# Hybrid attention and mLSTM layer: tiles at other addresses modulo 256, and all output products 256 columns wide

## The chip, the cores and the metric

The kernel runs on one core of one Trainium2 chip. TensorE (PE) multiplies matrices from SBUF into PSUM; VectorE (DVE), ScalarE (ACT) and GpSimd (POOL) do the rest; SyncE (SP) issues most DMAs. The metric is the device time of one execution in microseconds (us), taken as the median of several runs.

## What is computed

One decoder layer over 256 tokens of width 1024, all in 32-bit floats:

```python
h = rmsnorm(x, g_pre)
q_a, k_a, v_a, g_a, x_m, z_m = split(h @ w_in)      # 1024 x 6144, six parts of 1024 columns
y_a = attention(q_a, k_a, v_a, rel_bias) * silu(g_a)            # 8 heads of 128, causal
x_c = silu(conv4(x_m) + conv_b)                                 # depthwise, 4 taps
q_m, k_m, v_m = blockdiag(x_c, wq), blockdiag(x_c, wk), blockdiag(x_m, wv)
h_m = headwise_layernorm(mlstm(q_m, k_m, v_m, gates))           # 4 heads of 256
y_m = (h_m + skip * x_c) * silu(z_m)
out = x + rmsnorm(concat(y_a, y_m) @ w_out, g_post)             # 2048 x 1024
```

With 256 tokens and attention blocks of 256, attention is plain causal attention with a bias by distance.

## The kernel before

**Products in three terms.** The two large projections multiply numbers split in two: `hi` is a value rounded to the type fp32r and `lo` is the rest, and a product is the sum of three: hi x hi, hi x lo, lo x hi. The weights come in 32 blocks of 128 x 2048 (24 of `w_in`, 8 of `w_out`), each by one DMA into a `raw` tile; ACT rounds it into `hi` (line 101), DVE subtracts into `lo` (line 111), in halves, some blocks ahead (`split_next`). Each of `raw`, `hi` and `lo` has three buffers.

**The input projection.** The first two blocks arrive in pieces together with x and are multiplied in `project_group` (line 580). The other 22 go through `project` (line 566): for each half m of a block, 24 products (3 terms x 8 row blocks), each with its own weight load of 128 x 128 and 256 moving columns. For most blocks the stationary operand is the weight (`hi` or `lo`) and the moving one the input (`hhi`, `hlo`); for the v blocks it is the other way round.

**Small products between them.** `evacuate` and the generators started with `spawn` run between the halves: every half is a slot, `run_side` lets each generator do its next step before the half's products are issued. So PE's order is written by hand: a few small products, then 24 projection products. The names in the profile: `vps` and `qps` (lines 331, 338) make the mLSTM's v and q from the convolution; `gp`, `gif`, `cp` (351, 358, 385) its gates; `sp`, `nps`, `ht` (395 to 443) its heads; `as` (460, 461) the attention scores, `atp` (480) their transposes, `ao` (491, 492) the attention's output. `nps` and the first three products of `ao` have fp32r operands, the other small ones four-byte floats, which PE takes in two instructions each (transposes in one).

**The output projection.** `multiply_out(j, p)` (line 667) multiplies two of the 16 row blocks into one of five PSUM banks. `pieces` gives each bank its 128 tokens and columns: three are 512 columns wide and two 256. For each of the 2 row blocks there are 3 terms, with the layer's activations (`ymh`, `yml` of the mLSTM half; `yah`, `yal` of attention) stationary and the weights moving. Eight blocks j go through two slots each; the first ones still have attention steps between them. At the end `finish` takes the mean square of each bank (ACT, DVE) and the root (POOL), and `store` scales, adds x and writes out.

**Where tiles lie.** SBUF tiles come from four pools laid one behind the other: `cst`, `wts`, `wrk`, `big`. Inside a pool a tile (or a tag, which several tiles use in turn) takes the next address in the order of first request, rounded up to 32 bytes. `pad(n)` requests n bytes in `cst` that nothing uses. Every slice that a projection product reads starts a multiple of 512 bytes into its tile, so an operand's address modulo 256 is its tile's.

Of the kernel before, what the change touches and what calls it, by code (L numbers as in the profile page):

```python
# [10 lines left out]
F32 = mybir.dt.float32  # L11
F32R = mybir.dt.float32r
AF = mybir.ActivationFunctionType
OP = mybir.AluOpType
# [3 lines left out]
P = 128  # L18
D = 1024
S = 256  # L20
# [29 lines left out]
def hybrid_layer(ctx, tc, x, xw, small, wide, bias_t, g_post, w_in, w_out, out):  # L50
    nc = tc.nc
    pe, act, dve, pool = nc.tensor, nc.scalar, nc.vector, nc.gpsimd
# [5 lines left out]
    def pad(n):  # L58
        cst.tile([P, n // 4], F32, name="pad%d" % n)
# [7 lines left out]
    def bank(name):  # L67
        return psm.tile([P, 512], F32, tag="bank", name=name)
# [4 lines left out]
    def half_kb(name, n):  # L73
        return wrk.tile([P, n], F32, tag="kb2", name=name, bufs=6)
# [40 lines left out]

    big = ctx.enter_context(tc.tile_pool(name="big", bufs=1))

    first = big.tile([P, 6144 + 8], F32, name="first")  # L120

    def third(i):
        return first[:, 2048 * i:2048 * (i + 1)].rearrange("p (k s) -> p k s", s=S)
# [41 lines left out]
    gcol = first[:, 6144:]  # L165
    xc = third(1)

    sq = big.tile([P, 4, 2, S], F32, tag="ym0", name="sq")
    part = big.tile([P, S], F32, tag="ym1v", name="part")

    def rms_squares(q):
# [35 lines left out]
    rcol = cst.tile([P, 2], F32, name="rcol")  # L207
# [21 lines left out]
    def rms_spread(dg):  # L229
# [6 lines left out]
    bd = big.tile([P, 16, P], F32R, tag="ym0", name="bd").bitcast(F32)  # L236
    bda, bdv = bd[:, 0:8, :], bd[:, 8:16, :]
    bias = None
    xms = (big.tile([P, 6, S + 3], F32, tag="xm", name="xma"),
           big.tile([P, 2, S + 3], F32, tag="xmv", name="xmb"))  # L240

    def xm(f, n=1):
        t, f = (xms[0], f) if f < 6 else (xms[1], f - 6)
        return t[:, f, :] if n == 1 else t[:, f:f + n, :]

    v1h = big.tile([P, 2, MH, EH + 2], F32R, tag="v1", name="v1h")
    v1l = big.tile([P, 2, MH, EH + 2], F32R, name="v1l")

    tmp = big.tile([P, 1280], F32, tag="ym1", name="tmp")
    tmpv = big.tile([P, 576], F32, tag="ym1v", name="tmpv")  # L250

    wkr = tmp[:, 0:128]
    wifr = tmp[:, 128:896].rearrange("p (i n) -> p i n", i=3)
# [39 lines left out]
    def spawn(gen, at):  # L293
        side.append([at, gen])
# [15 lines left out]
    def conv(c, ps):  # L310
        dve.tensor_tensor(xm(2 * c, 2)[:, :, 3:], ps, rb2, OP.mult)
        yield CONV[c]
        cv = half_kb("cv", 512).rearrange("p (i n) -> p i n", n=S)
        for i in range(2):
            f = 2 * c + i
            act.activation(cv[:, i], xm(f)[:, 0:S], AF.Copy, scale=cols[:, 8 + f:9 + f])
        yield 1
        for i in range(2):
            f = 2 * c + i
            for j in range(1, 4):  # L320
                dve.scalar_tensor_tensor(cv[:, i], xm(f)[:, j:j + S],  # L321
                                         cols[:, 8 + 8 * j + f:9 + 8 * j + f], cv[:, i],
                                         op0=OP.mult, op1=OP.add)
            yield 1
            act.activation(xc[:, f, :], cv[:, i], AF.Silu, bias=cols[:, 40 + f:41 + f])  # L325
        yield VWAIT
        vps = bank("vps").rearrange("p (t n) -> p t n", n=EH)
        for t in range(2):
            for i in range(2):
                f = 2 * c + i  # L330
                pe.matmul(vps[:, t, i * P:(i + 1) * P], xm(f)[:, 3 + t * P:3 + (t + 1) * P],  # L331
                          bdv[:, f, :], start=True, stop=True)
        act.copy(v1h[:, :, c, 0:EH], vps)
        yield 1
        dve.tensor_tensor(v1l[:, :, c, 0:EH], vps, v1h[:, :, c, 0:EH].bitcast(F32), OP.subtract)
        qps = bank("qps").rearrange("p (a n) -> p a n", n=S)
        for i in range(2):
            pe.matmul(qps[:, i, :], bda[:, 2 * c + i, :], xc[:, 2 * c + i, :], start=True, stop=True)  # L338
        act.copy(qp[:, 2 * c:2 * c + 2, :], qps)

    pad(576)

    def row(name):
        return cst.tile([MH, S], F32, name=name)
# [103 lines left out]

    gs, yah = {}, {}
    yal = cst.tile([P, 8, S], F32R, name="yal")  # L450
    ym = {}
    gq = {}
    rb2 = rbc.unsqueeze(1).to_broadcast([P, 2, S])

    def attend(h):
        g, v0 = gq[h // 2]
        qt, kt, v1 = g[:, 0:2], g[:, 2:4], g[:, 4]
        i = h % 2
        sp = bank("as")
        pe.matmul(sp[:, 0:S], qt[:, i, P:], kt[:, i, :], start=True, stop=True)  # L460
        pe.matmul(sp[:, S:384], qt[:, i, 0:P], kt[:, i, 0:P], start=True, stop=True)  # L461
        e = half_kb("ae", 384)
        mn = wrk.tile([P, 2], F32, name="amn")
        rs = wrk.tile([P, 2], F32, name="ars")
        parts = ((0, 0, S), (1, S, 384))
        for a, o, z in parts:
            dve.tensor_tensor_reduce(e[:, o:z], sp[:, o:z], bias[:, h, S - (z - o):], -1.0, 3.0e38,  # L467
                                     OP.add, OP.min, mn[:, a:a + 1])
        yield 1
        for a, o, z in parts:  # L470
            act.activation(e[:, o:z], e[:, o:z], AF.Exp, scale=-1.0, bias=mn[:, a:a + 1],
                           accum_out=rs[:, a:a + 1])
        yield 1
        dve.reciprocal(rs, rs)
        for a, o, z in parts:
            dve.tensor_scalar(e[:, o:z], e[:, o:z], rs[:, a:a + 1], None, op0=OP.mult)
        yield 1
        tp = bank("atp")
        for n, o in enumerate((S, 0, P)):
            pe.transpose(tp[:, n * P:(n + 1) * P], e[:, o:o + P], ident)  # L480
        pt = wrk.tile([P, 2, S], F32R, tag="gsplit", name="apt", bufs=PBUF)
        p1 = half_kb("ap1", P)
        act.copy(pt[:, 0], tp[:, 0:S])  # L483
        act.copy(p1, tp[:, S:384])
        yield 1
        dve.tensor_tensor(pt[:, 1], tp[:, 0:S], pt[:, 0].bitcast(F32), OP.subtract)
        yield 1
        op = bank("ao")
        vs = slice(i * P, (i + 1) * P)
        for n, (a, b) in enumerate(((0, 0), (1, 0), (0, 1))):  # L490
            pe.matmul(op[:, 0:S], v0[:, a, vs], pt[:, b], start=n == 0, stop=False)  # L491
        pe.matmul(op[:, P:S], v1[:, vs], p1, start=False, stop=True)  # L492
        y = half_kb("ay", S)
        dve.tensor_tensor(y, op[:, 0:S], gs[h], OP.mult)
        yield 1
        yah[h] = big.tile([P, S], F32R, tag="ya%d" % h, name="yah")
        act.copy(yah[h], y)
        yield 1
        dve.tensor_tensor(yal[:, h, :], y, yah[h].bitcast(F32), OP.subtract)
# [26 lines left out]
    def evacuate(n, ps, slot):  # L526
        kind, c, _ = chunks[n]
        if kind == "m":
            spawn(conv(c, ps), slot)
            if c == 3:  # L530
                spawn(gates(), slot + GATES)
                for h in range(MH):
                    spawn(mlstm_head(h), slot + HEADS + HSTEP * h)
        elif kind == "z":
            spawn(gate_z(c, ps), slot)
        else:
            if kind == "g":
                spawn(gate_a(c, ps), slot)
            elif kind == "q":
                tag = ("ym1", "xm")[c % 2]  # L540
                gq[c] = (big.tile([P, 5, S], F32, tag=tag, name="qkv"),
                         big.tile([P, 2, S], F32R, tag=tag + "v", name="v0"))
                dve.scalar_tensor_tensor(gq[c][0][:, 0:2], ps, P ** -0.5, rb2, op0=OP.mult, op1=OP.mult)
            elif kind == "k":
                dve.tensor_tensor(gq[c][0][:, 2:4], ps, rb2, OP.mult)
            else:
                g, v = gq[c]
                act.activation(v[:, 0], ps[:, 0], AF.Copy, scale=rcol[:, 0:1])
                act.activation(g[:, 4], ps[:, 1], AF.Copy, scale=rcol[:, 1:2])
                dve.scalar_tensor_tensor(v[:, 1], ps[:, 0], rcol[:, 0:1], v[:, 0].bitcast(F32),  # L550
                                         op0=OP.mult, op1=OP.subtract)
                spawn(attend(2 * c), slot + 1)
                spawn(attend(2 * c + 1), slot + ASTEP)
# [60 lines left out]
    for n in range(2, NIN):  # L614
        ps = proj_bank()
# [42 lines left out]
    acc = []  # L658

    def multiply_out(j, p):  # L660
        n = NIN + j
        t, c, w = pieces[p]
        for i in range(2):
            f = (order[j] + i) % 8
            yh, yl = (yah[f], yal[:, f]) if order[j] < 8 else (ym["h"][:, f], ym["l"][:, f])
            for q, (yt, wt) in enumerate(((yh, his[n]), (yl, his[n]), (yh, los[n]))):
                pe.matmul(acc[p][:, 0:w], yt[:, t * P:(t + 1) * P], wt[:, i * D + c:i * D + c + w],  # L667
                          start=j == 0 and i == 0 and q == 0, stop=j == 7 and i == 1 and q == 2)

    steps = [(((j,), (0, 1)), ((j,), (2, 3, 4))) for j in range(6)]  # L670
    steps += [(((6,), (0, 1)), ((7,), (0, 1))), (((6, 7), (2,)), ((6, 7), (3, 4)))]
# [23 lines left out]
    for j in range(8):  # L695
        for m in range(2):
# [3 lines left out]
            if not acc:  # L700
                acc = [bank("acc%d" % p) for p in range(5)]
            js, ps = steps[j][m]
# [113 lines left out]
```

## Time and profile before

| | us |
|---|---|
| median of 3 runs (228.36 to 228.82) | 228.61 |
| the profiled execution | 228.33 |
| its span, first to last instruction | 226.6 |
| PE busy | 219.2 |
| DVE busy | 161.4 |
| ACT busy | 128.2 |
| POOL busy | 29.4 |

The profile is of one execution. A product's listed duration contains its way through the array and overlaps the next one's, so the distance between the starts of two products, or the length of a piece of the chain over its count, tells what a product costs. PE means products and PEld their weight loads.

### The profile page before, as it was taken

To read this page: it belongs to the slowest core of one execution; us is meant where nothing else is said; L and a number is where in the kernel's file an instruction comes from. 1 tells how busy PE (TensorE), PEld (TensorE's weight loads), DVE (VectorE), ACT (ScalarE), POOL (GpSimd) and SP (SyncE) were. 2 spreads that over 40 slices of the span, in tenths; PEclk is the share of its full clock that TensorE was granted. 3 is DMA by queue.
4 is the path that set the end of the run, shared out by engine and by line. 5 is a ranking of instruction groups with operands and counts; after the bars stand their busy time and mean duration, and the time that the engine had idled before them with its cause. 6 is when DMAs were issued, how large, how long until landed. Compare 5 with 4: busy or idle time off the path is not lost.

```text
span 226.6 us, 4213 instructions
## 1 busy us (share of the span) xinstructions
PE 219.2 (97%) x1688; PEld 209.0 (92%) x1688; DVE 161.4 (71%) x321; ACT 128.2 (57%) x228; POOL 29.4 (13%) x49
## 2 busy tenths in 40 slices
PE   8999999999999999999999999999999999999980
PEld 8999999999889999999999999999998888888870
DVE  1787999999935967384698898997773665464163
ACT  4787525877469464552656575996445634432220
POOL 2001394000000212000316154000000000000010
PEclk9999999999999999999999999999999999999996
DMA  6999594244545199425050440455545743740022
GB/s 197 406 420 373 197 353 147 74 178 174 194 179 188 15 302 327 149 90 188 0 189 0 185 159 30 185 188 185 188 187 185 268 140 150 275 187 3 0 93 94
DMA packets 7027, 39.90 MB, mean 176 GB/s; under 512 B 796, under 2 KB 1312, under 8 KB 3040
## 3 DMA queue, kind: packets, MB, share of 16 engines
q1 hardware_dynamic: 6608, 38.65, 46.1%
q0 software_dynamic: 256, 0.79, 1.5%
q8 instruction: 13, 0.21, 0.4%
q10 hardware_dynamic: 144, 0.20, 0.2%
q14 instruction: 6, 0.05, 0.1%
HBM read 38.58 MB, written 1.05 MB: 175 GB/s over the span
## 4 chain that ended last, share of the span: by engine, by line
PE 94%; issue 2%; DVE 1%; ACT 0%; POOLq 0%; POOL 0%; DVEq 0%
PE proj L566 54%; PE acc L667 17%; PE proj L580 5%; PE wake L160 2%; PE nps L416 2%; PE vps L331 2%; PE as L460 2%; PE sp L395 2%; PE qps L338 2%; PE ao L491 1%; PE atp L480 1%; PE gp L351 1%; PE sp L398 1%; PE as L461 1%; PE ao L492 1%
## 5 line engine op out<-in xcount | busy, mean ns | idle before, releaser
L111 DVE TENSOR_TENSOR lo<-raw,hi 128x1024 fp32r<-128x1024 f32 x60 | 72.5, 1225 | 3.3 <-ACT hi L101 3.3
L101 ACT CAST hi<-raw 128x1024 fp32r<-128x1024 f32 x60 | 61.6, 1046 | 12.4 <-issue 7.6
L566 PE MATMUL proj<-hhi,hi 128*128 128x256 f32 x288 | 41.7, 288 | 0.0
L566 PE MATMUL proj<-hlo,hi 128*128 128x256 f32 x288 | 39.5, 280 | 0.0
L566 PE MATMUL proj<-hhi,lo 128*128 128x256 f32 x288 | 39.3, 279 | 0.0
L566 PEld LDWEIGHTS proj<-hhi,hi 128*128 128x128 f32 x288 | 36.4, 189 | 1.0 <-issue 0.8
L566 PEld LDWEIGHTS proj<-hlo,hi 128*128 128x128 f32 x288 | 36.1, 189 | 0.1
L566 PEld LDWEIGHTS proj<-hhi,lo 128*128 128x128 f32 x288 | 36.0, 189 | 0.0
L667 PE MATMUL acc<-hi,ymh 128*128 128x512 f32 (+1 forms) x40 | 14.3, 357 | 0.0
L667 PE MATMUL acc<-hi,yah 128*128 128x512 f32 (+1 forms) x40 | 14.0, 350 | 0.0
L667 PE MATMUL acc<-hi,yml 128*128 128x512 f32 (+1 forms) x40 | 14.0, 350 | 0.0
L667 PE MATMUL acc<-lo,ymh 128*128 128x512 f32 (+1 forms) x40 | 14.0, 350 | 0.0
L667 PE MATMUL acc<-lo,yah 128*128 128x512 f32 (+1 forms) x40 | 14.0, 349 | 0.0
L667 PE MATMUL acc<-hi,yal 128*128 128x512 f32 (+1 forms) x40 | 13.9, 349 | 0.0
L686 POOL TENSOR_TENSOR oms<-oms,nhalf 128x1 f32<-128x1 f32 x2 | 1.1, 567 | 80.4 <-DVE oms L683 80.4
L483 ACT CAST apt<-atp 128x256 fp32r<-128x256 f32 x8 | 3.0, 370 | 13.8 <-PE atp L480 13.4
L325 ACT ACTIVATE first<-cv,sm 128x256 f32<-128x256 f32 x8 | 4.1, 510 | 9.8 <-DVE cv L321 9.8
L438 POOL TENSOR_SCALAR first<-first,sm 128x256 f32<-128x256 f32 x8 | 9.6, 1205 | 0.0
L679 ACT ACTIVATE sq<-acc 128x512 f32<-128x512 f32 (+1 forms) x5 | 2.6, 511 | 12.3 <-PE acc L667 12.3
L467 DVE CUSTOM_DVE_ANT_0 ae<-as,first 128x256 f32<-128x256 f32 (+1 forms) x16 | 5.0, 353 | 5.7 <-PE as L461 5.7
L566 PE MATMUL proj<-hi,hhi 128*128 128x256 f32 x64 | 9.1, 284 | 0.0
L321 DVE SCALAR_TENSOR_TENSOR cv<-xma,sm,cv 128x256 f32<-128x256 f32 x18 | 8.8, 488 | 0.4
(170 smaller groups left out, 388.3 us busy)
## 6 DMA issues: line engine op xcount, KB each, us to landing
raw<-in_w_in_dram SPq DMA_DIRECT2D x22, 1024.0 KB, 4.9
raw<-in_w_out_dram SPq DMA_DIRECT2D x8, 1024.0 KB, 4.8
first<-in_xw_dram SPq DMA_DIRECT2D x2, 768.0 KB, 7.9
first<-in_xw_dram SPq DMA_DIRECT2D x2, 512.0 KB, 5.1
first<-in_bias_dram SPq DMA_DIRECT2D x1, 1024.0 KB, 8.1
first<-in_x_dram SPq DMA_DIRECT2D x1, 1024.0 KB, 7.0
dl<-mdr POOLq DMA_DIRECT2D x1, 512.0 KB, 6.2
go<-in_g_post_dram SPq DMA_DIRECT2D x1, 512.0 KB, 7.8
```

What stands on the lines that cost most here:

```text
L101: act.copy(his[n][:, sl], raws[n][:, sl])
L111: dve.tensor_tensor(los[n][:, sl], raws[n][:, sl], his[n][:, sl].bitcast(F32), OP.subtract)
L160: pe.matmul(wk[:, 0:P], one, one, start=True, stop=True)
L321: dve.scalar_tensor_tensor(cv[:, i], xm(f)[:, j:j + S], cols[:, 8 + 8 * j + f:9 + 8 * j + f], cv[:, i], op0=OP.mult, op1=OP.add)
L331: pe.matmul(vps[:, t, i * P:(i + 1) * P], xm(f)[:, 3 + t * P:3 + (t + 1) * P], bdv[:, f, :], start=True, stop=True)
L338: pe.matmul(qps[:, i, :], bda[:, 2 * c + i, :], xc[:, 2 * c + i, :], start=True, stop=True)
L395: pe.matmul(sp[:, 0:S], xc[:, f, 0:P], qp[:, f, :], start=i == 0, stop=i == 1)
L438: pool.tensor_scalar(u[:, f, :], xc[:, f, :], cols[:, 56 + f:57 + f], None, op0=OP.mult)
L467: dve.tensor_tensor_reduce(e[:, o:z], sp[:, o:z], bias[:, h, S - (z - o):], -1.0, 3.0e38, OP.add, OP.min, mn[:, a:a + 1])
L566: pe.matmul(ps[:, m, :], a, b, start=first and j == ks[0] and k == 0, stop=last and j == ks[-1] and k == KT - 1)
L580: pe.matmul(ps[:, i, :], wt[:, k, i * P:(i + 1) * P], ht[:, k, :], start=k == 0 and i == 0 and j == 0, stop=k == 7 and i == 1 and j == 2, ...
L667: pe.matmul(acc[p][:, 0:w], yt[:, t * P:(t + 1) * P], wt[:, i * D + c:i * D + c + w], start=j == 0 and i == 0 and q == 0, stop=j == 7 and ...
```

## The change

Two things. Gaps of 32 to 224 bytes are put between the tags of `big` (a new helper `big_pad`), one pad of `cst` is cut by 64 bytes and 64 bytes are put behind `yal`; the tile of q, k and v gets 8 unused floats ahead of v (the second half of v's tokens), and `tmp`, which shares its buffer, grows likewise. And in `multiply_out` every product covers 256 columns: a 512-wide one becomes two with the same stationary operand, issued one behind the other.

Addresses modulo 256, added up from the sizes in order of request:

| tile | before | after |
|---|---|---|
| `hhi`, `hlo`; `xc`, `qp` and other parts of `first`; `gsplit`, `apt`; `ident` | 160 | 160 |
| `hi`, `lo`, `raw` | 224 | 224 |
| `sq`, `bd`, `yml` (tag `ym0`) | 192 | 32 |
| `part`, `tmpv`, `v0` of even pairs (tag `ym1v`) | 192 | 224 |
| `xma`, q and k of odd pairs (tag `xm`); `tmp`, q and k of even pairs, `go` (tag `ym1`) | 192 | 192 |
| `xmb`, `v0` of odd pairs (tag `xmv`) | 32 | 224 |
| `v1h`, `ymh` (tag `v1`) | 64 | 32 |
| `v1l` | 128 | 96 |
| `gs`, `yah` (tags `ya0` to `ya7`) | 192 | 32 |
| `yal` | 96 | 32 |
| v of the second half of the tokens, `g[:, 4]` | 192 | 224 |
| small scratch tiles (`ae`, `ap1`, `hn`, ...) | 32 | 32 |

```diff
@@ -115,6 +115,11 @@
+    def big_pad(n, gaps=[]):
+        gaps.append(n)
+        big.tile([P, n // 4], F32, name="gap%d" % len(gaps))
@@ -165,7 +170,9 @@
+    big_pad(96)
     sq = big.tile([P, 4, 2, S], F32, tag="ym0", name="sq")
+    big_pad(192)
     part = big.tile([P, S], F32, tag="ym1v", name="part")
@@ -236,18 +243,23 @@
-    xms = (big.tile([P, 6, S + 3], F32, tag="xm", name="xma"),
-           big.tile([P, 2, S + 3], F32, tag="xmv", name="xmb"))
+    big_pad(224)
+    xma = big.tile([P, 6, S + 3], F32, tag="xm", name="xma")
+    big_pad(192)
+    xms = xma, big.tile([P, 2, S + 3], F32, tag="xmv", name="xmb")
...
+    big_pad(32)
     v1h = big.tile([P, 2, MH, EH + 2], F32R, tag="v1", name="v1h")
     v1l = big.tile([P, 2, MH, EH + 2], F32R, name="v1l")
 
-    tmp = big.tile([P, 1280], F32, tag="ym1", name="tmp")
+    big_pad(32)
+    tmp = big.tile([P, 1288], F32, tag="ym1", name="tmp")
     tmpv = big.tile([P, 576], F32, tag="ym1v", name="tmpv")
+    big_pad(64)
@@ -338,7 +350,7 @@
-    pad(576)
+    pad(512)
@@ -448,13 +460,14 @@
     yal = cst.tile([P, 8, S], F32R, name="yal")
+    pad(64)
...
-        qt, kt, v1 = g[:, 0:2], g[:, 2:4], g[:, 4]
+        qt, kt, v1 = g[0], g[1], g[2]
@@ -538,15 +551,16 @@
-                gq[c] = (big.tile([P, 5, S], F32, tag=tag, name="qkv"),
-                         big.tile([P, 2, S], F32R, tag=tag + "v", name="v0"))
+                g = big.tile([P, 5 * S + 8], F32, tag=tag, name="qkv")
+                gq[c] = ([g[:, o:o + 2 * S].rearrange("p (i s) -> p i s", s=S) for o in (0, 2 * S)] +
+                         [g[:, 4 * S + 8:]], big.tile([P, 2, S], F32R, tag=tag + "v", name="v0"))
...
@@ -664,8 +678,12 @@
-                pe.matmul(acc[p][:, 0:w], yt[:, t * P:(t + 1) * P], wt[:, i * D + c:i * D + c + w],
-                          start=j == 0 and i == 0 and q == 0, stop=j == 7 and i == 1 and q == 2)
+                for o in range(0, w, S):
+                    pe.matmul(acc[p][:, o:o + S], yt[:, t * P:(t + 1) * P],
+                              wt[:, i * D + c + o:i * D + c + o + S],
+                              start=j == 0 and i == 0 and q == 0 and o == 0,
+                              stop=j == 7 and i == 1 and q == 2 and o + S == w,
+                              skip_group_check=True)
```

The lines left out write and read q, k and v through `g[0]`, `g[1]` and `g[2]`.

## Rows read from the trace of the kernel before

**Rows 1.** The page: busy us of each engine, share of the span, instructions.

```profile
PE 219.2 (97%) x1688; PEld 209.0 (92%) x1688; DVE 161.4 (71%) x321; ACT 128.2 (57%) x228; POOL 29.4 (13%) x49
```

**Rows 2.** The page: the chain that ended last, shares by engine and by line.

```profile
PE 94%; issue 2%; DVE 1%; ACT 0%; POOLq 0%; POOL 0%; DVEq 0%
PE proj L566 54%; PE acc L667 17%; PE proj L580 5%; PE wake L160 2%; PE nps L416 2%; PE vps L331 2%; PE as L460 2%; PE sp L395 2%; PE qps L338 2%; PE ao L491 1%; PE atp L480 1%; PE gp L351 1%; PE sp L398 1%; PE as L461 1%; PE ao L492 1%
```

**Rows 3.** Waits of PE: us in total, times, longest.

```profile
PE wake L160 <- PEq L804: 0.8, 1, 0.8
```

**Rows 4.** Timeline after the last product: start us, us, engine, line, operation.

```profile
220.07 0.38 ACT L679 ACTIVATE sq<-acc 128x256 f32<-128x256 f32 x1 [0.88 <-PE acc L667]
...
221.47 1.54 DVE L690 SCALAR_TENSOR_TENSOR first<-first,oms 128x384 f32<-128x384 f32 x3 [0.34 <-POOL oms L686]
```

**Rows 5.** The chain in order of time, projection: start us, us, line, products.

```profile
24.34 13.19 PE proj L566 x112
...
38.42 2.76 PE proj L566 x24
...
82.67 5.46 PE proj L566 x48
...
155.24 16.97 PE proj L566 x144
```

**Rows 6.** Stretches of PE: from:to us, length, busy (instructions), granted clock, DMA.

```profile
142.06:155.24 13.18, 13.18 (x119) 1.00 0.58 200
155.24:172.20 16.96, 16.96 (x145) 1.00 0.53 194
```

**Rows 7.** The chain in order of time, attention steps and the projection behind them.

```profile
104.29 0.22 PE as L461 x2
104.51 2.75 PE proj L566 x24
107.26 1.08 PE nps L416 x9
108.34 0.36 PE ao L491 x3
108.70 0.22 PE ao L492 x2
108.92 2.83 PE proj L566 x24
```

**Rows 8.** Timeline near the end of the output projection.

```profile
211.73 0.39 PE L667 MATMUL acc<-hi,yal 128*128 128x512 f32 x1
...
216.81 0.40 PE L667 MATMUL acc<-lo,yah 128*128 128x512 f32 x1
...
217.05 0.28 PE L667 MATMUL acc<-hi,yah 128*128 128x256 f32 x1
...
219.76 0.27 PE L667 MATMUL acc<-lo,yah 128*128 128x256 f32 x1
```

**Rows 9.** Groups of PE by form, output projection, one of six of each width.

```profile
L667 PE MATMUL acc<-hi,ymh 128*128 128x512 f32 x24 | 9.8, 408 | 0.0
...
L667 PE MATMUL acc<-hi,yal 128*128 128x256 f32 x16 | 4.5, 282 | 0.0
```

**Rows 10.** The chain in order of time, small products of the convolution.

```profile
41.18 0.86 PE qps L338 x4
...
44.79 0.89 PE vps L331 x8
```

**Rows 11.** Stretches 28:36 and 36:44 us, their sum by engine.

```profile
sum 16.00, PE 16.00 PEld 15.90 DVE 15.65 ACT 8.24 POOL 8.55; mean PE 8.00 PEld 7.95 DVE 7.82 ACT 4.12 POOL 4.28
```

**Rows 12.** Timeline of DVE at 35 us.

```profile
35.08 1.21 DVE L111 TENSOR_TENSOR lo<-raw,hi 128x1024 fp32r<-128x1024 f32 x1
```

**Rows 13.** Timeline of PE at 36 us.

```profile
36.42 0.64 PE L566 MATMUL proj<-hhi,lo 128*128 128x256 f32 x4
```

**Rows 14.** The chain in order of time, output projection, two slots.

```profile
191.55 5.60 PE acc L667 x30
```

More of the change, by code (lines that the diff above doesn't have):

```diff
@@ L540, in evacuate @@
                 tag = ("ym1", "xm")[c % 2]
-                gq[c] = (big.tile([P, 5, S], F32, tag=tag, name="qkv"),
-                         big.tile([P, 2, S], F32R, tag=tag + "v", name="v0"))
-                dve.scalar_tensor_tensor(gq[c][0][:, 0:2], ps, P ** -0.5, rb2, op0=OP.mult, op1=OP.mult)
+                g = big.tile([P, 5 * S + 8], F32, tag=tag, name="qkv")
+                gq[c] = ([g[:, o:o + 2 * S].rearrange("p (i s) -> p i s", s=S) for o in (0, 2 * S)] +
+                         [g[:, 4 * S + 8:]], big.tile([P, 2, S], F32R, tag=tag + "v", name="v0"))
+                dve.scalar_tensor_tensor(gq[c][0][0], ps, P ** -0.5, rb2, op0=OP.mult, op1=OP.mult)
             elif kind == "k":
-                dve.tensor_tensor(gq[c][0][:, 2:4], ps, rb2, OP.mult)
+                dve.tensor_tensor(gq[c][0][1], ps, rb2, OP.mult)
             else:
@@ L548, in evacuate @@
                 act.activation(v[:, 0], ps[:, 0], AF.Copy, scale=rcol[:, 0:1])
-                act.activation(g[:, 4], ps[:, 1], AF.Copy, scale=rcol[:, 1:2])
+                act.activation(g[2], ps[:, 1], AF.Copy, scale=rcol[:, 1:2])
                 dve.scalar_tensor_tensor(v[:, 1], ps[:, 0], rcol[:, 0:1], v[:, 0].bitcast(F32),
```

## Prediction

> **What bounds the kernel now.** I read the page first. PE is busy for 97% of the span, DVE for 71%, ACT for 57% [rows 1]. The chain of waits says the same: PE 94%, the input projection's products 54% + 5%, the output projection's 17% [rows 2]. From the first projection product to the last output product PE runs without a gap that another engine caused; the list of waits shows one wait of PE in the whole run, 0.8 us at the start [rows 3]. So the time is the sum of PE's instructions, and every nanosecond of spacing between two products is a nanosecond of the kernel, plus a tail after the last product that the change does not touch: ACT, POOL and DVE finish 256 columns and two queues store [rows 4].
>
> The question is then what spacing a product has. The chain in order of time gives it, as length over count [rows 5]. 48 projection products take 5.46 us from 82.67, 113.8 ns each. But 112 of them take 13.19 us from 24.34, and 144 take 16.97 us from 155.24: 117.8 ns each. Same shape, same line, and the granted clock is 1.00, its upper level (2.4 GHz), in a window of mostly fast pieces and in the slow stretch [rows 6], so 4.0 ns of each product come from something else. There are two paces and little between: of the 37 pieces of 24 products after 38 us in that chain, 16 take 2.73 to 2.76 us and 21 take 2.83 us or more (a stretch of 48, 96 or 144 counts as 2, 4 or 6). A stretch that starts slow stays slow until a small product interrupts it (six pieces on end from 155.24).
>
> What sets the pace when projection products resume? After an `as` pair (line 460, 461) all six stretches are fast; after an `ao` group (491, 492) all three are slow [rows 7]. The tiles that PE reads there differ in address. All projection products keep a fixed distance between their two operands, modulo 256: moving 160, stationary 224 (for the v blocks the reverse), which is 64 either way. Output products have distances of 160 and 32 (ymh, yml) or 32 and 128 (yah, yal), and none of their stretches has the fast pace: 256-wide ones start every 117.8 ns (217.05 to 219.76, 23 intervals), 512-wide ones every 231 ns (211.73 to 216.81, 22 intervals) [rows 8]. I read this as two read streams that get in each other's way by an amount that depends on their distance; the trace holds no address, so that step is inference.
>
> **The change part by part.** *512-wide products cut in two.* There are 144 of them (6 groups of 24), beside 96 (6 of 16) that are 256 wide already [rows 9]. After the change 384 products are 256 wide. If they keep the slow pace, each cut costs 2 x 117.8 - 231 = 4.6 ns, together +0.66 us [rows 8, 9]. If they run at 113.8, it gives 2 x 113.8 - 231 = -3.4 ns, -0.49 us, and the 96 others give 4.0 ns each, -0.38 us: together -0.87 us. These are the two ends. I take the fast one, because by the change all of them get stationary at 32 and moving at 224, a distance of 64, the only distance at which the trace has the fast pace at all. The 144 further weight loads are counted in these paces: each projection product has one too.
>
> *Attention's products.* `ao` has 24 products of 120 ns (0.36 us for 3) [rows 7]; v0 moves to 224 and the probabilities stay at 160, so their distance becomes 64. At 113.8 that is -0.15 us; the other end is 0. The `nps` group needs 1.08 us for 9, 120 ns each [rows 7]; its v1l part (12 products) comes to a distance of 64 or near it, its v1h part does not: between 0 and -0.2 us, I take -0.05.
>
> *Small products with four-byte operands* (`vps`, `qps`, `as`, `gp`): a `qps` group of 4 takes 0.86 us, a `vps` group of 8 takes 0.89 us [rows 10]. That is 215 and 111 ns each, with only one value across the run: nothing to win by themselves, and I take 0. What can move is the pace of the projection stretch behind them. Behind products whose tiles move, 12 pieces are slow (45.68, 49.38, 53.09, 62.29, 108.92, 135.84 and the six from 155.24) and three fast (38.42, 42.04, 56.79); a piece is worth 24 x 4.0 = 0.10 us. Ends: -1.2 us if all turn fast, +0.3 us if the three are lost. The nearest rows are the `ao` entries, whose last product has a distance of 96 now and gets 64. With a third of the slow ones turned, and none lost, -0.4 us.
>
> *What could take the gain back.* In 28 to 44 us DVE is busy for 15.65 of 16 us [rows 11]. DVE's second half of one lo block ends at 35.08 + 1.21 = 36.29 and PE's first product with it starts at 36.42 [rows 12, 13], 0.13 us later. A faster PE would wait there, so the slow stretch from 24.34 can give at most some 0.1 to 0.2 us of its 112 x 4.0 = 0.45. Nothing of the -0.4 stands on it. Gaps between tiles, `pad` values and views issue no instruction; the queues of SP and POOL get the same DMAs in the same order, and addresses of the DMA targets `raw`, `first` and `go` keep their remainder.
>
> *Sum.* -0.87 - 0.15 - 0.05 - 0.4 = -1.5 us. The profiled execution took 228.33 us (span 226.6, 1.7 around it), 0.28 below the median of the runs, 228.61. From its own time that gives 226.8, against the median 227.1, which I predict.
>
> A rule of the Trainium skill speaks against all this: "SBUF — State Buffer", section "SBUF: two separate sides", has PE never waiting on anyone, and "TensorE: Matmul & The Clock Gate", "What happens when you issue a matmul", gives the weight load a read port of its own. By its section "Back-to-back issue gap" a warm product costs N/2.4 + 2.5 ns, 109.2 for 256 columns, whatever the address, and 144 further products would cost 144 x 2.5 = 0.36 us, an estimate from that page: 229.0. The trace does not agree: the same instruction takes 113.8 and 117.8 ns at one granted clock.
>
> **The rivals.**
> *Addresses do not set the pace, or every entry of the output stage lands slow* (slower). Then all of the stage keeps 117.8 ns and the cut costs +0.66 us, all else equal: 229.3. For it: each pace also occurs at one and the same pair of addresses, so a distance of 64 permits the fast pace and does not force it; the start of a stretch decides, and the stretch from 197.73 alone holds half of the stage. Against it: no output stretch is fast now at distances other than 64. It decides when less than 0.66 / (0.66 + 0.87) = 43% of the stage's products run fast, with the projection unchanged.
> *Half and half* (no change): half of the stage fast gives about -0.1 us; `ao` and `nps` give -0.2; the projection stays: 228.3. For it: 16 of 37 pieces are fast now, near a coin.
> *Nearly every entry turns fast*: the output stage -0.87, attention -0.2, all 21 slow pieces -2.1, the early stretch -0.2 at most because of DVE: -3.4, 225.2. For it: the `as` entries show that a small product can bring the fast pace every time. Against it: `atp`, `sp`, `cp` and `gif` keep their tiles, and behind `atp` both paces occur.
>
> **How the numbers follow.** Forecast 227.1 with its own range 226.2 to 227.9: 0.46. Nearly every entry fast: 0.18. Half and half: 0.17. Slow output stage: 0.19. The measurement tells a difference from none at about 0.2%, 0.46 us. Faster by more: the first two and some of the third, 0.67. Within: 0.15. Slower by more: most of the last, 0.18. The range runs from 225.2, near the third rival, to 229.1, which takes in the half case and part of the slow one; about 2 in 10 stay outside, nearly all of it above.
>
> **What the changed profile would show.** Right: the output line is one form, 384 products, its stretches in the chain at 113 to 114 ns per product (30 products become 48, in 5.46 us instead of 5.60 [rows 14]); the `ao` groups 0.34 us for 3; more pieces of 24 in the projection at 2.73 to 2.76 us, first of all behind `ao`; no new waits of PE; the tail after the last product as long as now. Wrong: output stretches at 117.8 ns (5.65 us for 48), so the cut only costs; or projection stretches that were fast at 38 to 57 us now at 2.83, which would take back 0.1 us each; or PE waiting for a lo block near 36 us.

## The result and the profile after

The changed kernel takes 226.20 us (median of 4 runs, 225.71 to 226.56) against 228.72 us before in the same comparison: a ratio of 0.9892, with a 95% interval from 0.9877 to 0.9907, or 2.5 us less. The prediction was 227.1 us. The profiled execution took 226.29 us, its span is 224.6 us. The two profiled executions differ by 2.0 us and the medians by 2.5, since the one before ran 0.4 us below its median (228.33 against 228.72).

The page's first part answers to [rows 1]: 144 more products and weight loads, and less time in PE.

```profile
PE 216.7 (96%) x1832; PEld 212.3 (95%) x1832; DVE 162.0 (72%) x321; ACT 128.1 (57%) x228; POOL 29.2 (13%) x49
```

The chain in order of time (start us, length us, line, products) answers to [rows 5, 7, 10, 14]. Lines of the kernel have moved: the projection is 580, the output projection 682, attention 473 to 505.

```profile
35.85 1.14 DVE lo L111
36.99 0.04 issue
37.03 0.74 PE proj L580 x4
...
38.66 2.83 PE proj L580 x24
...
67.19 11.10 PE proj L580 x96
...
103.75 0.22 PE as L474 x2
103.97 2.83 PE proj L580 x24
106.80 1.09 PE nps L428 x9
107.89 0.35 PE ao L504 x3
108.24 0.22 PE ao L505 x2
108.46 2.74 PE proj L580 x24
...
154.72 16.34 PE proj L580 x144
171.06 2.72 PE acc L682 x24
...
174.44 5.46 PE acc L682 x48
...
189.99 5.66 PE acc L682 x48
...
196.23 16.35 PE acc L682 x144
```

Read length over count. The stretch of 144 projection products that took 16.97 us takes 16.34, 113.5 ns a product instead of 117.8. The output stage now consists of products of one form, and its stretches too run at 113 to 114 ns (16.35 us for 144), but for one of 48 that takes 5.66 us. A last stretch of 48 stands behind the 144 of that chain, which leaves PE for the tail at 212.58 us; it is fast as well. Behind `ao` the projection is fast (2.74 us), and behind `as` at 103.97 it is slow (2.83), each the other way round than before. And the chain goes through DVE up to 37 us, which it did not before.

The timeline (start us, length us) shows that place and the end, and answers to [rows 8, 12, 13].

```profile
35.77 1.21 DVE L111 TENSOR_TENSOR lo<-raw,hi 128x1024 fp32r<-128x1024 f32 x1
...
36.32 1.46 PE L580 MATMUL proj<-hhi,lo 128*128 128x256 f32 x8
...
217.73 0.28 PE L682 MATMUL acc<-lo,yah 128*128 128x256 f32 x1
```

Eight products from 36.32 take 1.46 us; eight of the same stretch ahead of them take 1.07. The missing 0.4 us is PE waiting for the half of a lo block that DVE finishes at 36.98. The second half of a block holds its row blocks 4 to 7, so it is the last four of the eight products that need it: the x4 at 37.03 in the chain.

Where the 2.0 us of the two spans lie, by the chain's times: up to the `vps` at 37.5 us the changed kernel is 0.24 us late (37.77 against 37.53; it comes out of the start 0.35 us later, the stretch from 24.3 us is 0.48 faster, the wait takes 0.39), from there to the output stage it needs 133.29 us instead of 134.67 (-1.38), from there to the start of the last product 46.67 instead of 47.56 (-0.89), and the tail is as long as before (6.9 against 6.8).

### The profile page after: what moved, and what is told of

It reads as the page before. It is cut to its first block, busy times and chain, and to the rows that moved or that the text cites. A ratio compares the mean times of both kernels' runs of the same rounds, so it can differ in the third digit from the quotient of the medians.

```text
span 224.6 us, 4502 instructions
## 1 busy us (share of the span) xinstructions
PE 216.7 (96%) x1832; PEld 212.3 (95%) x1832; DVE 162.0 (72%) x321; ACT 128.1 (57%) x228; POOL 29.2 (13%) x49
## 4 chain that ended last, share of the span: by engine, by line
PE 78%; DVE 6%; issue 3%; ACT 0%; POOLq 0%; POOL 0%; DVEq 0%
PE proj L580 46%; PE acc L682 17%; DVE lo L111 2%; PE nps L428 2%; PE vps L343 2%; PE as L473 2%; PE sp L407 2%; PE qps L350 2%; PE ao L504 1%; PE atp L493 1%; DVE xma L323 1%; PE gp L363 1%; PE sp L410 1%; PE as L474 1%; PE ao L505 1%
## 5 line engine op out<-in xcount | busy, mean ns | idle before, releaser
L682 PE MATMUL acc<-hi,ymh 128*128 128x256 f32 x64 | 14.2, 283 | 0.0
L682 PE MATMUL acc<-hi,yah 128*128 128x256 f32 x64 | 13.9, 277 | 0.0
L682 PE MATMUL acc<-hi,yml 128*128 128x256 f32 x64 | 13.8, 277 | 0.0
L682 PE MATMUL acc<-lo,ymh 128*128 128x256 f32 x64 | 13.8, 278 | 0.0
L682 PE MATMUL acc<-lo,yah 128*128 128x256 f32 x64 | 13.8, 276 | 0.0
L682 PE MATMUL acc<-hi,yal 128*128 128x256 f32 x64 | 13.8, 276 | 0.0
L682 PEld LDWEIGHTS acc<-hi,yml 128*128 128x128 f32 x64 | 10.3, 188 | 0.0
L682 PEld LDWEIGHTS acc<-hi,ymh 128*128 128x128 f32 x64 | 10.3, 189 | 0.0
L682 PEld LDWEIGHTS acc<-lo,ymh 128*128 128x128 f32 x64 | 10.3, 188 | 0.0
L682 PEld LDWEIGHTS acc<-lo,yah 128*128 128x128 f32 x64 | 10.2, 188 | 0.0
```

What stands on the lines that cost most here:

```text
L682: pe.matmul(acc[p][:, o:o + S], yt[:, t * P:(t + 1) * P], wt[:, i * D + c + o:i * D + c + o + S], start=j == 0 and i == 0 and q == 0 and o ...
```

## The experiments

Twelve kernels, each with five rounds against the kernel before. Ratios are to the kernel before; the changed kernel is at 0.9892. "Remainder" is an address modulo 256, "distance" that of the moving and the stationary operand modulo 256, taken the shorter way (the 160 of the prediction is 96 so).

### The cut alone, and the addresses alone

The kernel before with the change's last hunk, and the changed kernel without it.

> The kernel before with the 512-wide output products cut in two, every address as before. Theory (the distance between the two operands modulo 256 permits or forbids the fast pace): distances in the output stage stay at 32, 128 and 160, so all its products run at about 118 ns; the cut costs 144 x 4.6 = 0.66 us, 229.4 us. Rival (256 columns instead of 512 give the pace, not the address): the stage runs at 113 to 114 ns, about 0.9 us less than before, 227.8 us.

> The changed kernel with 512-wide output products back, all addresses as changed. Theory: distance sets the cost per column, so a 512-wide product takes 2 x 113.6 = 227 ns or a little less, and the time is that of the changed kernel, 226.2 us, within 0.3. Rival (the cut is needed for the fast pace): 231 ns per 512 columns remain, 144 x 4 = 0.6 us more, 226.8 us.

Cut alone: 229.46 us, ratio 1.0032 (1.0020 to 1.0044), slower by 0.7 us. Addresses alone: 226.93 us, ratio 0.9918 (0.9898 to 0.9938). The last long piece of the output stage in the chain, first of the cut alone:

```profile
198.15 17.10 PE acc L668 x144
```

of the addresses alone, with the stage's first piece:

```profile
171.16 2.79 PE acc L681 x12
...
196.56 16.75 PE acc L681 x84
```

At the old distances a 256-wide product takes 118.8 ns, so the cut only costs: the theory's number. But at a distance of 64 twelve 512-wide products take 2.79 us, 232 ns each, as much as before (231). There my theory fell and its rival held: the address does nothing for a 512-wide product. The products that were 256 wide already do gain from the address alone. The last ones of the addresses alone, in the timeline:

```profile
216.16 0.28 PE L681 MATMUL acc<-lo,yah 128*128 128x256 f32 x1
...
218.54 0.28 PE L681 MATMUL acc<-lo,yah 128*128 128x256 f32 x1
```

That is 113 ns each over 21 intervals, against 117.8 before. From the first to the last product the stage takes 47.56 us before, 48.29 with the cut alone, 47.38 with the addresses alone and 46.67 with both: most of the gain needs both.

### The output projection's tiles alone

The kernel before with the cut, and the four activation tiles at remainder 32; convolution and attention untouched.

```diff
-            ym["h"] = big.tile([P, 8, S], F32R, tag="v1", name="ymh")
-            ym["l"] = big.tile([P, 8, S], F32R, tag="ym0", name="yml")
+            ymh = big.tile([P, 2128], F32R, tag="v1", name="ymh")
+            yml = big.tile([P, 2112], F32R, tag="ym0", name="yml")
+            ym["h"] = ymh[:, 56:2104].rearrange("p (f s) -> p f s", s=S)
+            ym["l"] = yml[:, 24:2072].rearrange("p (f s) -> p f s", s=S)
```

with `big_pad(96)` ahead of the `ya` tags and `yal` as in the change.

> The kernel before with the cut and with the output projection's four activation tiles alone at remainder 32; convolution and attention tiles at the addresses of before (the block-diagonal weights share a buffer with yml but keep 192). Theory in two parts (distance 64 permits the fast pace, the small product ahead decides): output stretches behind the scores (72 products) fast, behind attention outputs (the last 192, and the one that starts as the projection's continuation) slow; the stage costs 0 to 0.4 us more than before, projection as before: 228.5 to 229.2 us. Rival (distance 64 alone is enough): the whole stage at 113.6 ns, 0.9 us less than before, 227.8 us.

227.66 us, ratio 0.9951 (0.9937 to 0.9964): 1.1 us less than before. The chain:

```profile
155.05 16.97 PE proj L575 x144
...
197.18 16.36 PE acc L677 x144
```

The projection is as slow as before, the output stage as fast as in the changed kernel. Both stretches stand right behind an attention output (of two different heads) with its old addresses; one is slow, the other fast. So the small product ahead does not decide by itself, and the rival's time came out. The stage takes 46.68 us, as in the changed kernel. The change has two parts that add: 1.1 us here, and 1.4 us in the projection (0.9951 against 0.9892).

### Other distances in the output stage

The changed kernel with the stage's stationary tiles moved together, by the same means as above. The weights stay at 224.

> The changed kernel with the output projection's stationary tiles all at remainder 96 instead of 32, a distance of 128 to the weights at 224. Theory (distance decides): no fast stretch in the output stage, 336 products that are fast now cost 4 to 5 ns more each, 1.5 us, 227.7 us. Rival (any common remainder will do, or the cut is what helps): 226.2 us.

> The same with the stationary tiles at remainder 224, a distance of 0 to the weights. Theory as I have it (only 64 either way permits the fast pace): slow, 118 ns or more, 227.7 us. If the distance acts as two streams meeting at the same place, 0 could be worse than 128: up to 122 ns, 229 us. Rival (any common remainder will do): 226.2 us.

> The same with the stationary tiles at remainder 160, a distance of 64 to the weights the other way round, as the v blocks of the input projection have it. Theory: the fast pace occurs as it does for v blocks, 226.2 us if the stretches start fast, 227.7 us if they all start slow; each stretch is at one of the two paces. Rival (only the changed kernel's own direction works): all slow.

> The changed kernel with the output projection's stationary tiles at remainder 0, 32 bytes beside the 32 of the changed kernel (distance 224 instead of 192, that is 32). Theory (the pace depends on the distance in steps finer than 64): between 113.6 and the 119.9 ns of distance 0, no stretch at the fast pace, 227.8 us. Rival (steps of 64 matter, 0 and 32 lie in the same one): as the changed kernel, 226.2 us.

The last long piece in each chain: remainder 96 (distance 128),

```profile
197.08 17.10 PE acc L683 x144
```

224 (distance 0),

```profile
197.85 17.28 PE acc L684 x144
```

160 (64 the other way), with the stage's first piece,

```profile
170.08 2.72 PE acc L684 x24
...
195.70 16.98 PE acc L684 x144
```

and 0 (distance 32):

```profile
197.05 17.05 PE acc L684 x144
```

| remainder | distance | ns per product in that piece | us | ratio (95%) |
|---|---|---|---|---|
| 32 (the change) | 64 | 113.5 | 226.20 | 0.9892 (0.9877 to 0.9907) |
| 160 | 64, other way | 117.9 | 227.33 | 0.9938 (0.9915 to 0.9961) |
| 0 | 32 | 118.4 | 227.74 | 0.9960 (0.9948 to 0.9973) |
| 96 | 128 | 118.8 | 227.84 | 0.9958 (0.9944 to 0.9972) |
| 224 | 0 | 120.0 | 228.26 | 0.9982 (0.9967 to 0.9998) |

Nothing but the addresses differs between these kernels, so they set the pace: 32 bytes off costs 1.5 us. A common remainder alone does not help. As the weights stay at 224, this table alone could also mean that the stationary tile's own remainder counts. Against that stands the projection: there a stationary tile at 224, the slowest remainder here, is fast with its moving tile at 160. So it is the pair that counts. The fast pace was seen at 64 only; the other way round it came in the first stretch (2.72 us for 24), which continues a projection stretch, and in none of the five behind small products. It is not shut out there: the v blocks of the projection have their 64 this way round too, and two of their pieces in the kernel before (118.31 and 122.35, 2.73 us each) are fast behind small products.

### What makes a projection stretch start fast

Three kernels take one address of the changed kernel back: `v1` to 192, `v0` to 192, the block-diagonal weights `bd` to 192.

```diff
-                         [g[:, 4 * S + 8:]], big.tile([P, 2, S], F32R, tag=tag + "v", name="v0"))
+                         [g[:, 4 * S:5 * S]], big.tile([P, 2, S], F32R, tag=tag + "v", name="v0"))
```

The other two use a longer tile and a slice of it, as above.

> The changed kernel with one address taken back: v of the second half of the tokens at remainder 192 instead of 224, so the last small product of each attention output (line 505) has its operands at 32 and 192 again. Theory (the last small product ahead of a stretch decides its pace by its own two addresses): all stretches right behind such a product turn slow, that is 2 pieces of 24, the stretch of 168 from 154.5 us and the stretch of 192 at the end, 408 products x 4.3 ns = 1.8 us more, 228.0 us. Rival (the three fp32r products before it decide, or chance): those stretches stay fast, 226.2 us within 0.4.

> The changed kernel with v0, the stationary operand of the three fp32r products of an attention output, at remainder 192 again (distance 32 instead of 64). Theory, new after the run that put v back (the pace carries over from the fp32r products through the small four-byte one): the projection stretches behind attention outputs turn slow, 2 pieces of 24 and the 144 from 154.5 us, 192 x 4.4 ns = 0.8 us, and the attention outputs themselves lose 0.1 us: 227.1 us. Rival (those stretches are set by something else, the timing or a later load): they stay fast, 226.3 us.

> The changed kernel with the block-diagonal weights, an operand of vps and qps, at remainder 192 again. Theory (the small product ahead decides): the stretches from 38 to 57 us show the order of the kernel before (fast, fast, slow, slow, slow, fast), and those behind gp, gif and cp (24, 96 and 24 products) turn slow as before, together up to 0.7 us more, 226.9 us; everything behind 82 us as in the changed kernel. Rival: no stretch behind gp, gif or cp changes, since their own operands don't, 226.2 us.

`v1` back: 226.98 us, ratio 0.9917 (0.9898 to 0.9937). The stretches behind `ao`:

```profile
109.12 2.76 PE proj L580 x24
...
136.24 2.83 PE proj L580 x24
...
155.60 16.36 PE proj L580 x144
```

`v0` back: 225.90 us, 0.9883 (0.9863 to 0.9903):

```profile
107.98 2.83 PE proj L581 x24
...
112.78 2.75 PE proj L581 x24
...
134.98 2.74 PE proj L581 x24
...
154.29 16.34 PE proj L581 x144
...
189.56 5.46 PE acc L683 x48
```

Each turns one short stretch right behind `ao` slow, not the same one, and the long stretch stays fast both times. Neither the last small product nor the three before it decide alone; both theories fell. Other stretches turned as well: with `v1` back one behind `atp` is slow (127.92 us, 2.83); with `v0` back the slow output stretch of the changed kernel is fast (5.46 us for 48 at 189.56, against 5.66), although a group of transposes stands between it and the `ao` that reads `v0`. And with `v0` back the piece at 112.78 is fast, which is slow in the changed kernel (113.17). Between it and the piece at 107.98 stand only `sp` and `as`, whose tiles did not move; what differs is that the piece ahead of them ran slow instead of fast. So the pace in front of the small products counts too. With `v1` back the profile is also 0.6 us later than the changed kernel's when the stretch behind `rp` starts, before any attention, so its time says less than its pieces.

`bd` back: 226.94 us, 0.9918 (0.9903 to 0.9933), 0.6 us more than the changed kernel by the ratios, whose intervals overlap at their edges:

```profile
46.10 2.83 PE proj L581 x24
48.93 0.86 PE qps L351 x4
49.79 2.83 PE proj L581 x24
...
53.51 2.83 PE proj L581 x24
...
66.50 0.96 PE gif L371 x4
67.46 11.52 PE proj L581 x96
...
155.49 16.34 PE proj L581 x144
```

The convolution's order of before is back (three slow pieces in a row, where the changed kernel has one), and so is the slow stretch behind `gif` (11.52 us for 96, as before, against 11.10), although no operand of `gif` moved (the `qps` ahead of `gif` reads `bd`); only behind `gp` the piece stays fast, against the expectation. From 82 us on all is as in the changed kernel. From the first `vps` to the first `as` the chain takes 44.39 us, against 43.80 in the changed kernel and 44.49 before, so this one address is worth about 0.6 us of the 1.4.

One more transposition ahead of the slow output stretch asks whether its start is a matter of timing.

```diff
+        if h == 7:
+            pe.transpose(tp[:, 384:], e[:, P:S], ident)
```

> The changed kernel with one more transposition, into unused columns, behind the last head's three: one product of 109 ns ahead of the only slow output stretch (48 products from 190.0 us). No address of the stretch or of the products ahead changes. Theory (the start of a stretch, a matter of timing, decides between the two paces that a distance of 64 permits): the stretch may turn fast, 5.46 instead of 5.66 us, and 0.1 us is paid, 226.1 us. Rival (the addresses ahead decide alone): it stays at 5.66 us, 226.3 us. The time can't tell these apart; the stretch in the profile does.

226.06 us, ratio 0.9883 (0.9870 to 0.9896), and the stretch stays slow:

```profile
190.10 5.66 PE acc L684 x48
```

Starting 0.1 us later changed nothing here, as the rival had it. From 45 us on the order of fast and slow pieces is the same in the profiles of all kernels that share the projection's and attention's addresses, although they get there up to 1.6 us apart.

Ahead of 45 us it is not the same, so timing is not ruled out. This kernel and the one with `v0` back have the same addresses modulo 256 there, and both come to `ss` (the sum of squares for the norm) at the fast pace. The chain of this kernel:

```profile
20.92 0.47 PE ss L221 x4
21.39 2.85 PE proj L582 x24
...
24.67 13.19 PE proj L582 x112
```

and with `v0` back:

```profile
20.98 0.34 PE ss L221 x4
21.32 2.93 PE proj L581 x24
...
24.68 12.71 PE proj L581 x112
```

Here `ss` took 0.13 us longer, the piece behind it is fast (1.07 us per eight products in the timeline, against 1.10), and the stretch of 112 behind `rp` is slow, where the other is fast. Behind `rp` all eleven profiles with the changed kernel's early addresses have the pace that the piece ahead of `rp` did not have: seven turn fast, four slow. So in these profiles the pace in front of a small product and a delay at it count as well as addresses do. No run tests that by itself.

### DVE out of the way

The changed kernel with one number in `setup` changed, so that the effective gate weights come four slots later.

```diff
                                  blk.unsqueeze(2).to_broadcast([P, 32, 4]), OP.mult)
-        yield 1
+        yield 5
         weff = tmpv[:, 384:576].rearrange("p (i t g) -> p i t g", i=3, g=8)
```

> The changed kernel with DVE's effective gate weights (six instructions, about 3.7 us) four slots later, so that DVE is not late with a lo block near 37 us. Theory (the early stretch that has turned fast waits for DVE, so its gain is lost): the wait of about 0.4 us goes, and 225.8 us; if the later slots have no room on DVE it only moves. Rival (the wait costs nothing because something else is late): 226.2 us unchanged.

225.97 us, ratio 0.9878 (0.9856 to 0.9900). In the timeline the wait is gone; the eight products take 1.07 us:

```profile
33.23 1.21 DVE L111 TENSOR_TENSOR lo<-raw,hi 128x1024 fp32r<-128x1024 f32 x1
...
36.21 1.07 PE L580 MATMUL proj<-hhi,lo 128*128 128x256 f32 x8
```

The edit did this, as DVE starts as late as in the changed kernel here (the lo half at 28.13 us, against 28.08). The span is 0.6 us shorter (224.0 us), but the timed difference of 0.2 us to the changed kernel lies within both intervals. It beats the kernel before; whether it beats the changed one stays open.

## Why the prediction was right

**PE's spacing is the time.** Right: the tail is unchanged and the spans differ by what the chain's pieces differ by.

**The output stage.** Forecast -0.87, measured -0.89 by the two chains and -1.1 us timed with these tiles alone. 336 of 384 products run at the fast pace. The step that fast products need a distance of 64 is shown by the five remainders, as far as those go; that the cut costs 0.66 without it, by the cut alone (0.7). What I had not seen is that 512-wide products gain nothing from the distance.

**Attention's products.** Forecast -0.15 for `ao`; its groups take 0.34 to 0.36 us instead of 0.35 to 0.36, about -0.1 over eight groups. `nps` takes 1.08 to 1.10 us as before: 0 in place of -0.05.

**The projection behind small products.** This is the mis-sized term: -0.4 forecast (a third of the slow pieces behind moved tiles turned, and none lost), -0.6 with `ao` and `nps`, and the chain shows -1.38 for all three. Of the 37 pieces of 24 after 38 us 29 are fast instead of 16. Of the twelve slow pieces behind moved tiles eleven turned fast, and of the three fast ones one went the other way (now at 38.66). Behind tiles that did not move seven turned to the 113.5 ns pace (four behind `gif`, one behind `cp`, two behind `atp`) and four to the other (two behind `as`, one each behind `atp` and `sp`). So the reading "after `as` always fast, after `ao` always slow" described the kernel before and was no rule: the start depends on more than the two addresses of the small product ahead, and on the pace in front of it, which is how pieces behind unmoved tiles could turn. That most slow pieces would turn was not foreseen. The total lies at the fast end of the forecast's own range (226.2) by this term, and that it lies no further out is luck. Which address is behind the convolution's part is shown (`bd`); behind the attention part it stays open, as `v0` and `v1` were only put back one at a time.

**DVE as the cover's end.** PE waits 0.4 us for the lo block near 36 us, the place that was named, but the working does not hold. The 0.13 us of reserve was read off the first of the eight products; the fifth is the one that needs the block's second half, and it started at about 36.42 + 4 x 0.118 = 36.89, 0.60 us behind DVE's 36.29. A stretch that is 0.45 us faster fits into that: with `v0` back, and at remainder 160, it takes 12.71 us instead of 13.19 and PE does not wait, with DVE's program unchanged. The changed kernel waits because DVE was late from the start. The rounding of a block on ACT, which DVE's subtraction waits for, first before and then after (length behind the start, the wait in brackets):

```profile
19.11 2.00 ACT L101 CAST hi<-raw 128x1024 fp32r<-128x1024 f32 x2 [0.76 <-DVE sq L177]
```

```profile
19.87 2.00 ACT L101 CAST hi<-raw 128x1024 fp32r<-128x1024 f32 x2 [1.27 <-DMA raw<-in_w_in_dram]
```

A DMA landed later, and DVE's lo block at 36 us came 0.69 us later with it (35.77 against 35.08), PE at `rp` only 0.35 (24.09 against 23.74). That the stretch was fast at all hung on the start too: at the same addresses it is slow in four of eleven profiles. Moving DVE's other work away removes the wait where DVE is late.

**The rivals.** Addresses do set the pace, so the slower case did not come; nor did the one with every entry fast, as eight pieces and one output stretch are slow. Two of the forecast's signs of being wrong did show, each small: a stretch fast before is slow (38.66), and PE waits near 36 us. By the rule of the Trainium skill ("SBUF — State Buffer", "SBUF: two separate sides") that PE never waits on anyone the five remainders would have taken one time; they take from 226.20 to 228.26 us. The prediction's 109.2 ns leaves out what the Trainium skill ("TensorE: Matmul & The Clock Gate", "Back-to-back issue gap") says beside it: the formula is for an isolated product, and in a stream of weight loads and products both set the spacing. Here each product has a weight load of its own.

**What is argued only.** That the moving and the stationary stream meet in the memory is the simplest reading of a dependence on their distance; no run shows the memory itself.

## What to carry to other kernels

Where PE is never idle, divide the length of a stretch by its products and compare stretches of the same shape: two paces at one granted clock are time to be had. Lay the moving and the stationary operand of fp32r products at a chosen distance modulo 256, measure the distance on the whole stage, and change width and address together, since each alone may lose or gain little. Compare several profiles of one program before a stretch's pace is put down to an edit: early in this kernel it differs between them at the same addresses. Then look for the engine that was just in time for the slower PE.

## What the runs showed of the hardware

A 256-column fp32r product took 113.5, 117.9, 118.4, 118.8 or 120.0 ns by the distance of its two operands modulo 256 and, at 64, by what ran ahead, at a granted clock of 1.00. At a distance of 64 two paces exist, 113.5 and 117.8 ns, and a stretch keeps the one it starts with for up to 192 products (the changed kernel from 196.23 us). A 512-column product took 231 to 233 ns at the old distances and at 64 alike, more than two fast products of 256 (227). Moving the operand of a small product (`bd`) changed the pace of a stretch of 96 products, although a small product with unmoved operands (`gif`) stands between them. At the same addresses the stretch of 112 products from 24.7 us took 12.71 or 13.19 us, by the pace of the piece ahead of it.
